# The first modulation's weights and the first norm's sums, in a hybrid diffusion trunk on Trainium2

## The chip, the cores and the metric

The program runs on one core of a Trainium2 chip. The metric is the device time of one execution in microseconds (us); lower is better. The engines are named as in the profile: PE (TensorE, matmuls), ACT (ScalarE), DVE (VectorE), POOL (GpSimd) and SP (SyncE, which issues loads).

## The reference

Two layers are computed for 128 context tokens and 512 latent tokens (640 together), with 1024 features, in float32. Only the beginning of the first layer is touched by the change:

```python
def modulation(cvec, w, b):
    m = jax.nn.silu(cvec) @ w + b
    return jnp.split(m[:, None, :], N_MOD, axis=-1)
...
sh1_p, sc1_p, g1_p, sh2_p, sc2_p, g2_p = modulation(c_ctx[None, :], mod_w, mod_b)
sh1_s, sc1_s, g1_s, sh2_s, sc2_s, g2_s = modulation(c, mod_w, mod_b)
hp = rms_norm(xp, norm1) * (1 + sc1_p) + sh1_p
hs = rms_norm(xs, norm1) * (1 + sc1_s) + sh1_s
```

`rms_norm` divides each token by the root of the mean of its squares over the 1024 features. The normed and modulated tokens go into one projection to queries, keys and values, then into attention, and so on through an MLP and a second layer.

## The kernel before

Tokens lie along the free axis and features along the 128 partitions: x is eight blocks (k = 0 to 7) of 128 x 640. A value that enters a large matmul is split into a rounded part, hi, and the rest, lo, so that each product is three matmuls (hi hi, hi lo, lo hi; lines 245 to 247 for the dense layers, 618 to 620 for `proj_step`).

The program has two phases. The first holds the attention layer; there a planner orders the instructions of each engine and of each queue by a timeline of its own, so that an instruction whose inputs and buffers are ready can be put ahead of one that was written earlier. The second phase (MLP, second layer) keeps the written order. The queues (SP's and ACT's loads among them) run in the order given to them. A load takes one of eight completion counters in turn and waits for the load that had that counter before.

`first_norm` (line 310) makes the eight blocks of hi and lo for the projection:

- It loads the eight x blocks on SP's queue (line 320), then the first 2048 columns of the modulation weights in four quarters w0 to w3 of 512 columns, 2 MB each (line 324), into three buffers, so that w3 waits for the buffer of w0. Behind w1 the call `use(None, None)` loads the first 256 projection columns, those of the keys and values (`proj_w`, line 608; line 611 is the load).
- `sumsq` (lines 295 to 299) squares each block on ACT and adds it into one tile `acc` on DVE. `rsqrt` (lines 306 to 308) multiplies `acc` by a matrix of ones, one matmul for each half of 320 tokens, which sums over the partitions and gives every partition the sum; Ln and Exp turn it into `rs`.
- For each quarter s, 32 small products (line 340, two records each) give the shifts and scales of blocks 2s and 2s + 1, a copy (343), a transpose (345) and a few tiny operations (348, 350) put them in place as the gain `g` and the shift.
- Then blocks 2s and 2s + 1 are scaled, shifted and split. Blocks 0 to 3 use one form: x times gain times `rs` on DVE (357), the rounded part with the shift added on ACT (358), the rest on DVE (359). Blocks 4 to 7 use another: x times `rs` on DVE (363), gain and shift on ACT for even blocks (369) and on DVE for odd ones (366), then a cast on ACT (235) and a subtract on DVE (236).
- `use(k, ...)` multiplies the block at once with the key/value columns, for five token blocks: 15 matmuls into three of the four `pj` banks of PSUM. The fourth, and the two `md` banks after the last modulation product, take the next 256 columns, which `proj` loads, splits and multiplies.

After it the kv banks are evacuated: `split_v` (605, 606), `qknorm` (681 to 686) and `rotated` (700 to 708), which needs tables built from `rope` (loaded on ACT's queue at line 662, used at 668 and 673). `cka` and `cv` (713, 715) are the context keys and values of the same stage, `vall` (711) holds the values. The pools `m0` (w) and `np` (acc, sq, rs) are closed when `first_norm` ends, and the memory behind the earlier tiles is then given to the pools `qkv`, `akq` and `qt` in this order; `rope` is the first tile of `qt`.

Of the kernel before, what the change touches and what calls it, by code (L numbers as in the profile page):

```python
# [18 lines left out]
P = 128  # L19
D = 1024  # L20
# [29 lines left out]
class Net:  # L50
# [259 lines left out]
    def first_norm(self, use):  # L310
# [3 lines left out]
        with ExitStack() as c:  # L314
# [3 lines left out]
            for k in range(NK):  # L318
                t = self.xp.tile([P, T], F32, tag="x", name="x")
                nc.sync.dma_start(out=t, in_=self.i["xT"][k * P:(k + 1) * P, :])  # L320
                xt.append(t)
            for s in range(4):
                wt = mp.tile([P, NK, 512], F32, tag="w", name="w")
                nc.sync.dma_start(out=wt, in_=w[:, s * 512:(s + 1) * 512].rearrange("(k p) c -> p k c", p=P))
                ws.append(wt)
                if s == 1:
                    use(None, None)
            for k in range(NK):
                self.sumsq(k, xt[k], 0, T)
            rs = self.np.tile([P, T], F32, tag="rs", name="rs", bufs=1)  # L330
            for hf in range(2):
                self.rsqrt(rs, hf, "kq")
            g = self.gain[0, 0]
            by_block = lambda z: z.rearrange("p (i k) -> p k i", i=2)
            for s in range(4):
# [11 lines left out]
                for v in range(2):  # L347
# [3 lines left out]
                                                   in1=self.vec("n1_0")[:, two], op0=ALU.add, op1=ALU.mult)  # L351
                for k in (2 * s, 2 * s + 1):
                    if k < 4:
                        x, (hi, lo) = xt[k], self.act[2 * k:2 * k + 2]
                        for v, o in ((0, slice(0, TS)), (1, slice(TS, T))):
                            sh = self.mod_vec(0, 0, k, v)
                            nc.vector.scalar_tensor_tensor(out=x[:, o], in0=x[:, o], scalar=g[:, k, v:v + 1], in1=rs[:, o], op0=ALU.mult, op1=ALU.mult)
                            nc.scalar.activation(hi[:, o], x[:, o], AF.Identity, bias=sh)
                            nc.vector.scalar_tensor_tensor(out=lo[:, o], in0=x[:, o], scalar=sh, in1=hi[:, o].bitcast(F32),
                                                           op0=ALU.add, op1=ALU.subtract)  # L360
                        use(k, (hi, lo))
                        continue
# [1382 lines left out]
```

## Time and profile before

| | us |
|---|---|
| three runs | 1806.48, 1808.74, 1809.97 |
| their median | 1808.74 |
| the profiled execution | 1806.72 |
| its span, from the first to the last instruction | 1805.0 |
| PE busy in it | 1726.7 |
| DVE, ACT busy in it | 1266.6, 921.0 |

The page of the profile gives the busy time of each engine over the whole span. The stretch that matters here is the first 60 us, so most of the reading is done with views that take a window: busy time by stretch, the timeline, the loads. Matmuls are pipelined, and their ends are modelled; a few per cent of the matmul records can be missing.

### The profile page before, as it was taken

The numbers are of one execution on the slowest core, as the hardware profiler recorded it, in microseconds if no ns is written. First come the engines' busy times: TensorE is split into PE (matmuls) and PEld (weight loads), VectorE is DVE, ScalarE is ACT, GpSimd is POOL, SyncE is SP. The second block draws the span as 40 slices with busy tenths as digits, with TensorE's granted clock in tenths as the row PEclk, the third lists the DMA queues.
The fourth block names the chain that finished last, engine by engine and source line by source line (L and its number), as shares of the span: only waits on it lengthen the run. The fifth ranks groups of instructions, "written<-read, shape, count | busy, mean of one in ns | idle before, by whom it ended". The sixth has DMA issues, their size and how long they took to land. (4 is left out here: it accounts for less than half of the span.)

```text
span 1805.0 us, 34898 instructions
## 1 busy us (share of the span) xinstructions
PE 1726.7 (96%) x14120; PEld 1621.2 (90%) x14120; DVE 1266.6 (70%) x2554; ACT 921.0 (51%) x2037; POOL 215.1 (12%) x218
## 2 busy tenths in 40 slices
PE   5999998899999999999989999999999999999999
PEld 4898886699999999999888878878999999999999
DVE  6766557469988678787697877776449957465562
ACT  4555565345345171554756656656636427164360
POOL 0233314100000000000232222222110000000000
PEclk9999998999999999999999999999999999999999
DMA  9101059314433435254122222232232423222231
GB/s 351 57 27 50 26 157 284 132 52 164 164 117 125 135 101 200 73 178 162 48 48 70 50 48 69 51 82 73 66 129 94 140 63 101 72 71 94 68 104 52
DMA packets 174994, 187.22 MB, mean 104 GB/s; under 512 B 48457, under 2 KB 152137, under 8 KB 174833
## 3 DMA queue, kind: packets, MB, share of 16 engines
q1 hardware_dynamic: 170272, 175.05, 30.9%
q0 software_dynamic: 1408, 5.41, 0.9%
q10 hardware_dynamic: 3152, 4.52, 0.8%
q8 instruction: 111, 1.82, 0.4%
q14 instruction: 51, 0.41, 0.1%
HBM read 170.97 MB, written 11.37 MB: 101 GB/s over the span
## 5 line engine op out<-in xcount | busy, mean ns | idle before, releaser
L228 ACT CAST t<-t 128x1024 fp32r<-128x1024 f32 x169 | 176.5, 1048 | 243.0 <-PE p L246 135.7
L229 DVE TENSOR_TENSOR t<-t 128x1024 fp32r<-128x1024 f32 x169 | 207.3, 1230 | 56.8 <-ACT t L228 55.9
L245 PE MATMUL dn<-t 128*128 128x320 f32 x648 | 207.7, 320 | 3.7 <-PEq L78 3.1
L246 PE MATMUL dn<-t 128*128 128x320 f32 x648 | 208.2, 321 | 0.0
L247 PE MATMUL dn<-t 128*128 128x320 f32 x648 | 207.4, 320 | 0.0
L246 PE MATMUL p<-hl,t 128*128 128x320 f32 x448 | 138.5, 309 | 0.0
L245 PEld LDWEIGHTS dn<-t 128*128 128x128 f32 x648 | 122.5, 189 | 7.9 <-issue 5.8
L246 PE MATMUL dn<-hl,t 128*128 128x320 f32 x416 | 129.0, 310 | 0.0
L192 DVE SCALAR_TENSOR_TENSOR ma<-t,ma 128x1024 f32<-128x1024 f32 x98 | 122.8, 1279 | 6.0 <-DMA t<-in_mod_w_dram 5.8
L246 PEld LDWEIGHTS dn<-t 128*128 128x128 f32 x648 | 122.6, 189 | 4.0 <-issue 2.5
L247 PEld LDWEIGHTS dn<-t 128*128 128x128 f32 x648 | 122.6, 189 | 3.4 <-issue 2.5
L413 DVE SCALAR_TENSOR_TENSOR x<-p,t,x 128x192 f32<-128x192 f32 (+2 forms) x154 | 53.1, 385 | 101.0 <-PE p L247 101.0
L245 PE MATMUL p<-hh,t 128*128 128x320 f32 x392 | 121.3, 310 | 0.0
L247 PE MATMUL p<-hh,t 128*128 128x320 f32 x392 | 121.2, 309 | 0.0
L245 PE MATMUL dn<-hh,t 128*128 128x320 f32 x376 | 116.8, 311 | 0.0
L247 PE MATMUL dn<-hh,t 128*128 128x320 f32 x376 | 116.2, 309 | 0.0
L228 ACT CAST wxh<-t 128x1024 fp32r<-128x1024 f32 x49 | 51.3, 1047 | 85.9 <-PE p L246 40.6
L413 DVE SCALAR_TENSOR_TENSOR x<-dn,t,x 128x320 f32<-128x320 f32 (+1 forms) x86 | 44.9, 525 | 62.4 <-PE dn L247 51.8
L246 PEld LDWEIGHTS p<-hl,t 128*128 128x128 f32 x448 | 84.1, 188 | 0.0
L246 PEld LDWEIGHTS dn<-hl,t 128*128 128x128 f32 x416 | 78.1, 188 | 1.0 <-issue 0.8
L783 POOL TENSOR_TENSOR p<-p,smx 128x640 f32<-128x640 f32 (+1 forms) x48 | 63.8, 1338 | 114.9 <-DVE smx L782 99.3
L245 PEld LDWEIGHTS p<-hh,t 128*128 128x128 f32 x392 | 73.6, 188 | 0.8 <-issue 0.4
(599 smaller groups left out, 5195.7 us busy)
## 6 DMA issues: line engine op xcount, KB each, us to landing
t<-in_mlp_w_dram SPq DMA_DIRECT2D x64, 1024.0 KB
t<-in_mod_w_dram SPq DMA_DIRECT2D x40, 1024.0 KB, 6.4
t<-in_w_qkv_dram SPq DMA_DIRECT2D x12, 1024.0 KB
t<-in_w_in_dram SPq DMA_DIRECT2D x9, 1024.0 KB, 5.4
w<-in_mod_w_dram SPq DMA_DIRECT2D x4, 2048.0 KB, 16.3
t<-in_w_out_dram SPq DMA_DIRECT2D x8, 1024.0 KB, 5.7
bias<-in_biasx_dram SPq DMA_DIRECT2D x8, 512.0 KB, 6.7
t<-in_w_z_dram SPq DMA_DIRECT2D x4, 1024.0 KB
```

Source lines behind the costliest of these rows:

```text
L192: nc.vector.scalar_tensor_tensor(out=acc[v], in0=wt[:, k], scalar=c, in1=acc[v], op0=ALU.mult, op1=ALU.add)
L228: nc.scalar.copy(hi, raw)
L229: nc.vector.tensor_tensor(out=lo, in0=raw, in1=hi.bitcast(F32), op=ALU.subtract)
L245: self.nc.tensor.matmul(ps, lhsT=hi[:, k, :], rhs=xh[:, ts_], start=(k == 0), stop=False)
L246: self.nc.tensor.matmul(ps, lhsT=hi[:, k, :], rhs=xl[:, ts_], start=False, stop=False)
L247: self.nc.tensor.matmul(ps, lhsT=lo[:, k, :], rhs=xh[:, ts_], start=False, stop=(k == NK - 1))
L413: nc.vector.scalar_tensor_tensor(out=xout[:, a:b], in0=ps[:, a - o:b - o], scalar=self.mod_vec(layer, idx, k, v), in1=xin[:, a:b], op0=ALU ...
L783: nc.gpsimd.tensor_tensor(out=pv, in0=pv, in1=sm.unsqueeze(2).broadcast_to([P, nb, w]), op=ALU.mult)
```

## The change

It touches `first_norm` and two loads in `attn_layer`. The first quarter of the modulation weights is loaded ahead of the x blocks, the projection columns come behind x, and the other three quarters behind them. The first modulation product is written ahead of the sums. The squares of blocks (0, 1), (2, 3) and (4, 5) are added in pairs on DVE, those of 6 and 7 are left single, and each of the five results is multiplied by the ones matrix into two PSUM banks that accumulate. `acc` is gone, `sq` has four buffers instead of two. All eight blocks use the form of blocks 0 to 3. The loads of `cka` and `cv` move from ACT's queue to SP's.

```diff
--- before.py
+++ after.py
@@ -315,24 +315,16 @@
             mp = c.enter_context(self.tc.tile_pool(name="m0", bufs=3))
             self.open_norm(c)
             xt, ws = [], []
-            for k in range(NK):
-                t = self.xp.tile([P, T], F32, tag="x", name="x")
-                nc.sync.dma_start(out=t, in_=self.i["xT"][k * P:(k + 1) * P, :])
-                xt.append(t)
-            for s in range(4):
+            g = self.gain[0, 0]
+            by_block = lambda z: z.rearrange("p (i k) -> p k i", i=2)
+
+            def load(s):
                 wt = mp.tile([P, NK, 512], F32, tag="w", name="w")
                 nc.sync.dma_start(out=wt, in_=w[:, s * 512:(s + 1) * 512].rearrange("(k p) c -> p k c", p=P))
                 ws.append(wt)
-                if s == 1:
-                    use(None, None)
-            for k in range(NK):
-                self.sumsq(k, xt[k], 0, T)
-            rs = self.np.tile([P, T], F32, tag="rs", name="rs", bufs=1)
-            for hf in range(2):
-                self.rsqrt(rs, hf, "kq")
-            g = self.gain[0, 0]
-            by_block = lambda z: z.rearrange("p (i k) -> p k i", i=2)
-            for s in range(4):
+
+            def modulation(s):
+
                 two = slice(2 * s, 2 * s + 2)
                 ps = self.bank("md")
                 for k in range(NK):
@@ -349,26 +341,44 @@
                                             in1=by_block(self.vec("modb0")[:, 0:16])[:, two], op=ALU.add)
                     nc.vector.scalar_tensor_tensor(out=g[:, two, v], in0=self.modT[0][:, 8 + 2 * s:10 + 2 * s, v], scalar=1.0,
                                                    in1=self.vec("n1_0")[:, two], op0=ALU.add, op1=ALU.mult)
+
+            load(0)
+            for k in range(NK):
+                t = self.xp.tile([P, T], F32, tag="x", name="x")
+                nc.sync.dma_start(out=t, in_=self.i["xT"][k * P:(k + 1) * P, :])
+                xt.append(t)
+            use(None, None)
+            for s in range(1, 4):
+                load(s)
+            modulation(0)
+
+            sums = [self.bank("kq")[:, 0:TH] for _ in range(2)]
+            for ks in ((0, 1), (2, 3), (4, 5), (6,), (7,)):
+                sq = []
+                for k in ks:
+                    sq.append(self.np.tile([P, T], F32, tag="sq", name="sq", bufs=4))
+                    nc.scalar.activation(sq[-1], xt[k], AF.Square)
+                if len(ks) == 2:
+                    nc.vector.tensor_tensor(out=sq[0], in0=sq[0], in1=sq[1], op=ALU.add)
+                for hf in range(2):
+                    nc.tensor.matmul(sums[hf], lhsT=self.ones, rhs=sq[0][:, hf * TH:(hf + 1) * TH], start=(ks[0] == 0), stop=(ks[0] == 7))
+            rs = self.np.tile([P, T], F32, tag="rs", name="rs", bufs=1)
+            for hf in range(2):
+                c = rs[:, hf * TH:(hf + 1) * TH]
+                nc.scalar.activation(c, sums[hf], AF.Ln, bias=self.eps, scale=1.0 / D)
+                nc.scalar.activation(c, c, AF.Exp, scale=-0.5)
+            for s in range(4):
+                if s:
+                    modulation(s)
                 for k in (2 * s, 2 * s + 1):
-                    if k < 4:
-                        x, (hi, lo) = xt[k], self.act[2 * k:2 * k + 2]
-                        for v, o in ((0, slice(0, TS)), (1, slice(TS, T))):
-                            sh = self.mod_vec(0, 0, k, v)
-                            nc.vector.scalar_tensor_tensor(out=x[:, o], in0=x[:, o], scalar=g[:, k, v:v + 1], in1=rs[:, o], op0=ALU.mult, op1=ALU.mult)
-                            nc.scalar.activation(hi[:, o], x[:, o], AF.Identity, bias=sh)
-                            nc.vector.scalar_tensor_tensor(out=lo[:, o], in0=x[:, o], scalar=sh, in1=hi[:, o].bitcast(F32),
-                                                           op0=ALU.add, op1=ALU.subtract)
-                        use(k, (hi, lo))
-                        continue
-                    nc.vector.tensor_tensor(out=xt[k], in0=xt[k], in1=rs, op=ALU.mult)
+                    x, (hi, lo) = xt[k], self.act[2 * k:2 * k + 2]
                     for v, o in ((0, slice(0, TS)), (1, slice(TS, T))):
-                        if k % 2:
-                            nc.vector.tensor_scalar(out=xt[k][:, o], in0=xt[k][:, o], scalar1=g[:, k, v:v + 1],
-                                                    scalar2=self.mod_vec(0, 0, k, v), op0=ALU.mult, op1=ALU.add)
-                        else:
-                            nc.scalar.activation(xt[k][:, o], xt[k][:, o], AF.Identity, scale=g[:, k, v:v + 1], bias=self.mod_vec(0, 0, k, v))
-                    use(k, self.split_act(k, xt[k]))
-            self.acc = None
+                        sh = self.mod_vec(0, 0, k, v)
+                        nc.vector.scalar_tensor_tensor(out=x[:, o], in0=x[:, o], scalar=g[:, k, v:v + 1], in1=rs[:, o], op0=ALU.mult, op1=ALU.mult)
+                        nc.scalar.activation(hi[:, o], x[:, o], AF.Identity, bias=sh)
+                        nc.vector.scalar_tensor_tensor(out=lo[:, o], in0=x[:, o], scalar=sh, in1=hi[:, o].bitcast(F32),
+                                                       op0=ALU.add, op1=ALU.subtract)
+                    use(k, (hi, lo))
         return [self.act[2 * k:2 * k + 2] for k in range(NK)]
 
     def norm_half(self, xt, layer, which, hf, tag="s1"):
@@ -710,9 +720,9 @@
 
             nc.scalar.dma_start(out=vall[:, 5, :], in_=I["ctxv"][:, 128:640])
             ck = tp.tile([P, KVA, 128], F32, name="cka", bufs=1)
-            nc.scalar.dma_start(out=ck, in_=I["ctxk"][:, 0:KVA])
+            nc.sync.dma_start(out=ck, in_=I["ctxk"][:, 0:KVA])
             cv = tp.tile([P, 128], F32, name="cv", bufs=1)
-            nc.scalar.dma_start(out=cv, in_=I["ctxv"][:, 0:128])
+            nc.sync.dma_start(out=cv, in_=I["ctxv"][:, 0:128])
             split_v(va[5], cv)
             kd = [tp.tile([P, KVA, 2, HD], F32, name=f"ka{blk}", bufs=1) for blk in range(NB)]
```

## Rows read from the trace of the kernel before

**Rows 1.** The page, part 1: TensorE's busy time, share of the span, instructions.
```profile
PE 1726.7 (96%) x14120; PEld 1621.2 (90%) x14120; DVE 1266.6 (70%) x2554; ACT 921.0 (51%) x2037; POOL 215.1 (12%) x218
```

**Rows 2.** Windows of the start: stretch, length, busy (instructions), granted clock, DMA share, GB/s.
```profile
4.50:6.00 1.50, 0.00 (x0) 0.00 (x0) 1.50 (x9) 0.00 (x0) 0.00 (x0) 1.00 0.96 267
17.80:41.40 23.60, 18.79 (x267) 16.59 (x267) 16.96 (x38) 9.67 (x17) 0.00 (x0) 0.93 1.06 373
24.00:27.00 3.00, 2.58 (x50) 2.13 (x40) 2.04 (x5) 1.76 (x4) 0.00 (x0) 0.50 1.07 371
44.00:58.00 14.00, 14.00 (x119) 13.97 (x117) 7.11 (x23) 5.64 (x15) 0.51 (x2) 1.00 0.15 47
58.00:75.00 17.00, 15.50 (x126) 14.92 (x125) 16.31 (x47) 9.94 (x38) 7.19 (x15) 1.00 0.24 70
```

**Rows 3.** Timeline, 14 to 42 us: start, length, engine, line, operation, count.
```profile
14.66 2.50 PE L306 MATMUL kq<-acc,t 128*128 128x320 f32 x4 [14.66 <-DVE acc L299]
...
16.13 0.53 ACT L307 ACTIVATE rs<-kq,t 128x320 f32<-128x320 f32 x1 [2.61 <-PE kq L306]
...
17.20 0.53 ACT L307 ACTIVATE rs<-kq,t 128x320 f32<-128x320 f32 x1
...
17.83 3.20 PE L340 MATMUL md<-w,t 128*32 128x128 f32 x64 [0.67 <-DMA w<-in_mod_w_dram]
...
22.25 1.94 DVE L357 SCALAR_TENSOR_TENSOR x<-x,t,rs 128x512 f32<-128x512 f32 x4
23.04 1.97 ACT L358 ACTIVATE t<-x,t 128x512 fp32r<-128x512 f32 x4 [1.66 <-DVE x L357]
...
23.36 3.22 PE L340 MATMUL md<-w,t 128*32 128x128 f32 x64 [1.54 <-DMA w<-in_mod_w_dram]
...
26.24 1.99 ACT L228 CAST t<-t 128x1024 fp32r<-128x1024 f32 x2 [1.24 <-DMA t<-in_w_in_dram]
...
27.34 0.62 PE L618 MATMUL pj<-t 128*128 128x256 f32 x3 [0.75 <-ACT t L228]
...
41.54 1.95 PE L340 MATMUL md<-w,t 128*32 128x128 f32 x64 [1.09 <-DMA w<-in_mod_w_dram]
```

**Rows 4.** Windows of the pj tiles alone, TensorE: busy time (matmuls) to 41.40.
```profile
0.00:41.40 41.40, 9.66 (x72) 0.96 1.00 353
```

**Rows 5.** DMA issues to 60 us: tile, queue, count, KB of each, median us to landing.
```profile
w<-in_mod_w_dram SPq DMA_DIRECT2D x4, 2048.0 KB, 16.3
t<-in_w_in_dram SPq DMA_DIRECT2D x4, 1024.0 KB, 14.7
x<-in_xT_dram SPq DMA_DIRECT2D x8, 320.0 KB, 6.1
rope<-in_rope_dram ACTq DMA_DIRECT2D x1, 256.0 KB, 2.8
...
cka<-in_ctxk_dram ACTq DMA_DIRECT2D x1, 128.0 KB, 3.3
cv<-in_ctxv_dram ACTq DMA_DIRECT2D x1, 64.0 KB, 5.0
```

**Rows 6.** Groups of ScalarE to 50 us, shapes apart: busy, mean ns, idle before.
```profile
L298 ACT ACTIVATE sq<-x 128x640 f32<-128x640 f32 x7 | 5.1, 736 | 1.5 <-DVE acc L299 0.8 <-DMA x<-in_xT_dram 0.8
...
L358 ACT ACTIVATE t<-x,t 128x512 fp32r<-128x512 f32 x4 | 2.8, 724 | 4.0 <-DVE x L357 4.0
```

**Rows 7.** Timeline of ScalarE and VectorE: rope's tables, a late load, the first kv evacuation.
```profile
4.43 0.42 DVE L668 TENSOR_TENSOR tbgqa_r<-rope,t 128x256 f32<-128x256 f32 x1 [0.40 <-DMA t<-in_vecs_dram]
...
5.65 0.62 DVE L673 TENSOR_TENSOR tbgkan_r<-rope,t 128x64 f32<-128x64 f32 x4
...
43.69 0.33 ACTq L711 DMA_DIRECT2D vall<-in_ctxv_dram  x1
...
53.66 0.27 ACT L605 CAST va<-pj 128x128 fp32r<-128x128 f32 x1 [5.81 <-PE pj L620]
...
57.44 0.29 DVE L700 TENSOR_TENSOR t<-kn,tbgkan_r 128x128 f32<-128x128 f32 x1
```

## The prediction

> **What bounds the kernel now.** I read the page first. TensorE (PE) is busy for 96% of the span [rows 1], so time is won only where PE idles, or where its work starts sooner. The windows show where it idles [rows 2]: 18.79 us busy of the 23.6 us from 17.80 to 41.40, and full, 14.00 of 14.00, from 44 to 58. In the first of these stretches the DMA engines' share is 1.06 at 373 GB/s: the start is bound by loading. The timeline shows in which order the loads let PE go [rows 3]. The sums of squares run at 14.66, each quarter w0 to w3 of the modulation product when its 2 MB land (17.83, 23.36, ..., 41.54), and the first key/value (kv) matmul at 27.34, as soon as the first 256 projection columns are cast (26.24; ACT had waited for that load). From 41.54 on PE has no gap; so the end of this stage is set by when w3 lands and by how many projection matmuls are left then. By 41.40, 72 of them were done [rows 4]; 119 matmuls in 14.00 us [rows 2] make 0.118 us for each one left.
>
> **The change, part by part.** *The order of loads.* Sizes are in [rows 5]: w 2.10 MB each, x 8 × 0.33, projection columns 1.05 each. The old queue had x, w0, w1, columns; the new one has w0, x, columns, w1, w2, w3. Ahead of the end of the first columns there are 2.10 MB (w1) and 0.45 MB (rope, cka, cv, if none of them stays in front) less: 2.55 MB at 373 GB/s are 6.8 us, so 26.2 becomes 19.4. Between 4.5 and 6.0 only 267 GB/s were moved [rows 2], while SP issued the eight small x loads; with 2 MB in front of them I expect the full rate, 0.16 MB or 0.4 us won: 19.0. By the same count w0 lands at 9.2 (6.2 MB less than the 8.3 that stand ahead of 26.2), the last x at 16.2 (3.6 MB less).
>
> w3 must wait for the buffer of w0 (three buffers). That is free once the first product is done, at about 13, so SP is not held there. But the planner, which puts each queue's instructions in the order in which they can run, had already put the second projection columns ahead of w3, and I expect it again; then the bytes ahead of w3 are the old ones less those of rope (0.26 MB, 0.7 us; see below). w3 lands 0.4 + 0.7 = 1.1 us sooner, at 40.4. Bounds: 0 (nothing won), and 3.9 (w3 ahead of those columns: another 1.05 MB, 2.8 us). I take 1.1, the order that the planner chose before.
>
> *The sums of squares.* Seven adds into acc on DVE become three; two ones-matmuls become ten. Two took 2.50 us, and their readers started 1.07 apart (16.13 and 17.20) [rows 3]; the first modulation product took 3.20 us against 1.95 for the fourth, so that pace is that of the lower level, 1.2 GHz. Ten cost 10.7 us at it, 5.4 at 2.4 GHz. They follow the first product (9.2 + 3.2 = 12.4), so they end between 18.7 (set by the last x at 16.2, its square of 0.74 [rows 6], a short queue and the last pair) and 23.1. I take 18.7, because PE then has work from 9.2 on with few gaps. After it come Ln and Exp (1.07 for each half by the two readers' distance, the first half partly under the last matmul, so some 1.6), the scale of block 0 (0.79, from 22.25 to 23.04) and its rounding (0.72 [rows 6]) with the handing over: the first kv matmul at 22.0 instead of 27.34. At worst it is 26.5.
>
> A rule of the Trainium skill speaks against this part: TensorE: Matmul & The Clock Gate, "Loop structure matters more than you think", calls a DMA wait between matmuls the bad loop, which leaves the array at the lower clock. By that rule the sums take the 10.7 us (cold sums, below). The trace agrees so far that the second product, after PE's wait for w1, took 3.22 us and the clock was granted at 0.50 from 24 to 27 [rows 2, 3].
>
> *What PE gets done before w3.* From 22.0 to 40.4 are 18.4 us. Off go the second and third product (1.95 each; w1 now lands at about 24.5) and one wait: from the end of a product to the first rounded block were 2.7 us (21.03 to 23.04 + 0.72 [rows 3, 6]), and blocks 0 and 1 are used up by then. An estimate of 0.5 for the two small transposes and their hand-overs goes off too. That leaves 11.3 us, or 95 matmuls, 23 more than the 72; at 0.118 that is 2.7 us. Bounds: with the sums at 1.2 GHz 13.9 us remain (26.5 to 40.4), less one product and 1.3 to 2.3 us of gaps, so 82 to 90: 1.2 to 2.1 us. At most 108 can be done (kv for six blocks, and the one block of the next columns that has a free bank): 4.2 us.
>
> *One form for all blocks.* Blocks 4 to 7 lose an early multiply by rs, a cast and a separate subtract, and take what blocks 0 to 3 had: 2.8 us for two blocks to be scaled and rounded (22.25 to 25.01 [rows 3]). The work on the last two blocks after w3 stays near its present length, and PE has the projections of the second columns (36 matmuls, 4.2 us, on the two md banks) to fill it: 0. If that filler had been used up, 2.8 us would show.
>
> *cka and cv* go from ACT's queue to SP's, 0.19 MB [rows 5], and wait behind w2 there, but in front of w3; nothing reads them before the last blocks are done: 0. At worst w3 is 0.5 us later than I count, were they moved from behind it.
>
> *Rope.* It is untouched, but its place is not. The tiles of this stage took 3 × 16 KB for w and 4 × 2.5 KB for acc, two sq and rs, 58 KB; the pools that come after (vall to kha) take 60, and rope begins behind them, so it was loaded at the start and its tables were built from 4.43 to 6.27 [rows 7]. Now there are four sq and rs: 60.5 KB. The last tile, rs, would reach into rope, and its load may only start when rs is read for the last time, at about 46 (40.4 + 1.95 + 2.7 for the first of the last two blocks, and the rest of them). For such an overlap the trace has an example: vall lies over w0's buffer, and its load was issued at 43.69, 0.2 us behind the end of the last product on it (41.54 + 1.95 [rows 3, 7]). Loads of this size landed 2.8 to 5.0 us after their issue [rows 5]. So rope lands at 49 to 51 and the tables (1.84 us of DVE) are ready near 52. The first rotation was at 57.44 [rows 7], and would now come near 53.6. It fits by a hair; I take 0, and the other end is the slower rival.
>
> **The sum.** 1.1 + 2.7 = 3.8 us less. The profiled execution took 1806.72 (span 1805.0), 2.0 below the median of 1808.74; from it comes 1802.9, and from the median **1804.9**. Its own range goes from 1.1 + 1.2 to 1.1 + 4.2: 1803.4 to 1806.4. Beyond 41 us PE was full until 58, so the lead is passed on, unless the planner shifts later work. About 0.2%, 3.6 us, is what can be told from no change, so this case lies on that line.
>
> **The rivals.** *A larger gain.* ACT waited 5.81 us, until 53.66, for the first finished kv bank [rows 7], while PE ran other projections. Then DVE was busy 16.31 of 17 us [rows 2]. If all six early blocks are in the banks before w3 lands, the evacuation starts up to 5.8 us sooner and DVE, the next limit there, with it: 1808.7 - 5.8 = 1802.9. For it: 22.0 is early. Against it: the planner interleaves.
>
> *Cold sums.* Each pair of ones-matmuls waits for its x blocks, PE's clock stays at 1.2 GHz as it did in the first product, and kv starts near 26.5: only 1.1 + 1.2 to 1.1 + 2.1 remain, about 1806.
>
> *Slower.* The rope load is issued by ACT, in order. If it stands behind the first copy out of a kv bank, which waited until 53.66, it lands near 58.5, the tables are ready at 60.4 instead of being there at 57.44, and their 1.84 us fall into the stretch where DVE has 0.7 us to spare: 3.0 + 1.84 = 4.8 us of loss, and PE's lead is then of no use: 1813.5. The point is whether the tables are ready when the first key is normed (57.44 now). Against it: the planner can put the issue before that copy.
>
> *It does not do what it says.* The planner leaves x ahead of w0, since all are ready at the start: 1808.7.
>
> **How the numbers follow.** Forecast 0.42, half of it beyond the line; larger gain 0.24; cold sums 0.12; slower 0.18; not done 0.04. Faster: 0.21 + 0.24 = 0.45; same: 0.21 + 0.12 + 0.04 = 0.37; slower 0.18. The range reaches from 1799, below the larger gain by the 3.9 us that w3 could come sooner, to 1813, nearly the whole of the slower case.
>
> **What would show it.** In the new timeline: the first product near 9.2, the last ones-matmul by 18.7, the first kv matmul near 22, the last product at 40.4, more than 90 matmuls into the pj banks before it, rope issued after the last scale and its tables done before the first rotation. I am wrong if the last product comes no sooner than 41, if PE idles after it, or if DVE stands at a rope table while a finished bank waits.

## The result and the profile after

The changed kernel took 1822.98 us in the median of four runs (1821.73 to 1825.38), the kernel before 1807.61 (1805.56 to 1809.97, four runs): a ratio of 1.0085, 95% interval 1.0066 to 1.0103. It is slower by 15 us where a gain was forecast, and lies above the predicted range (1799 to 1813). The profiled execution of the changed kernel took 1824.09 us with a span of 1822.4.

By the page's first part PE is busy for 13.5 us longer than in [rows 1] (1726.7), and idle for 3.9 us longer (82.2 of the span for 78.3). Of the longer busy time 4.4 us are the sums (3.47 and 3.40 us in the timeline below, for the 2.50 of before).

```profile
PE 1740.2 (95%) x14136; PEld 1629.8 (89%) x14136; DVE 1264.4 (69%) x2554; ACT 917.8 (50%) x2037; POOL 215.4 (12%) x218
```

The windows that answer to [rows 2] (stretch, length, busy time of PE, PEld, DVE, ACT and POOL with instructions, granted clock, DMA share, GB/s):

```profile
4.50:6.00 1.50, 0.00 (x0) 0.00 (x0) 0.00 (x0) 0.00 (x0) 0.00 (x0) 1.00 1.05 406
17.80:41.40 23.60, 18.27 (x208) 15.30 (x207) 13.91 (x32) 10.14 (x21) 0.00 (x0) 0.86 1.03 365
...
44.00:58.00 14.00, 14.00 (x140) 13.47 (x134) 7.27 (x29) 3.52 (x10) 0.00 (x0) 1.00 0.44 129
58.00:75.00 17.00, 12.63 (x92) 12.06 (x90) 15.40 (x46) 10.26 (x37) 5.84 (x14) 0.90 0.04 9
...
24.58:29.00 4.42, 4.42 (x38) 3.70 (x39) 2.23 (x6) 1.16 (x3) 0.00 (x0) 0.50 1.06 389
```

From 17.80 to 41.40 PE was busy for 0.5 us less than before and at a lower granted clock (0.86 for 0.93). From 44 to 58 it is full as before; behind that, from 58 to 75, it lacks 2.9 us of work.

The timeline of PE (start, length, line, operation, count; in brackets the idle time before and what ended it), which answers to [rows 3]:

```profile
9.90 3.64 PE L332 MATMUL md<-w,t 128*32 128x128 f32 x64 [9.90 <-DMA w<-in_mod_w_dram]
13.47 3.47 PE L364 MATMUL kq<-sq,t 128*128 128x320 f32 x8
...
16.89 3.40 PE L364 MATMUL kq<-sq,t 128*128 128x320 f32 x12
24.58 0.58 PE L628 MATMUL pj<-t 128*128 128x256 f32 x1 [4.30 <-ACT t L378]
...
26.15 1.92 PE L332 MATMUL md<-w,t 128*32 128x128 f32 x28
...
31.62 1.28 PE L332 MATMUL md<-w,t 128*32 128x128 f32 x36
...
33.53 1.95 PE L332 MATMUL md<-w,t 128*32 128x128 f32 x64
...
42.01 1.06 PE L332 MATMUL md<-w,t 128*32 128x128 f32 x26
...
43.67 0.64 PE L332 MATMUL md<-w,t 128*32 128x128 f32 x14
...
47.54 0.86 PE L332 MATMUL md<-w,t 128*32 128x128 f32 x24
...
49.15 0.27 PE L337 MATMUL md<-t,modm 128*128 128x128 f32 x1
...
62.73 0.33 PE L745 MATMUL kq<-t,ka 128*128 128x128 f32 x1 [3.24 <-DVE ka L718]
```

The loads did what was predicted: the first product at 9.90 instead of 17.83, the first kv matmul 2.8 us sooner than the 27.34 of before. But the second product, one piece at 23.36 before, begins at 26.15 and is cut in two by the kv matmuls of blocks 0 and 1; and the last, one piece at 41.54 before, is cut in three and ends at 48.40 instead of 43.49. PE has no gap there: it did kv matmuls in between. What the lead was meant to buy did not come either, as the window of the pj tiles shows (72 matmuls in [rows 4]):

```profile
0.00:41.40 41.40, 10.58 (x68) 0.92 0.98 346
```

The other engines pass the delay on. ACT and VectorE, answering to [rows 3, 7]:

```profile
19.43 1.99 ACT L228 CAST t<-t 128x1024 fp32r<-128x1024 f32 x2 [1.63 <-DMA t<-in_w_in_dram]
...
51.84 0.36 ACTq L672 DMA_DIRECT2D rope<-in_rope_dram  x1
...
55.10 0.50 ACT L609 CAST kha<-cka 128x128 fp32r<-128x128 f32 x2 [2.48 <-DMA cka<-in_ctxk_dram]
...
57.01 0.27 ACT L615 CAST va<-pj 128x128 fp32r<-128x128 f32 x1 [1.17 <-PE pj L630]
```

```profile
34.04 1.94 DVE L377 SCALAR_TENSOR_TENSOR x<-x,t,rs 128x512 f32<-128x512 f32 x4
...
49.86 1.94 DVE L377 SCALAR_TENSOR_TENSOR x<-x,t,rs 128x512 f32<-128x512 f32 x4
...
57.47 0.62 DVE L683 TENSOR_TENSOR tbgkan_r<-rope,t 128x64 f32<-128x64 f32 x4
...
61.40 0.29 DVE L710 TENSOR_TENSOR t<-kn,tbgkan_r 128x128 f32<-128x128 f32 x1
```

The rows of before that these are compared with, for blocks 2 and 3, the last transpose and the first key:

```profile
29.98 1.94 DVE L357 SCALAR_TENSOR_TENSOR x<-x,t,rs 128x512 f32<-128x512 f32 x4
...
44.48 0.27 PE L345 MATMUL md<-t,modm 128*128 128x128 f32 x1
...
58.78 0.33 PE L735 MATMUL kq<-t,ka 128*128 128x128 f32 x1 [0.60 <-DVE ka L708]
```

Blocks 2 and 3 are scaled at 34.04 (29.98 before), blocks 6 and 7 at 49.86 (45.41), the first kv bank is evacuated at 57.01 (53.66), the first key rotated at 61.40 (57.44). PE has done its spare projections by 59.5 and waits 3.24 us for that key, at a time when it had waited 0.60 before (until 58.78).

From there the delay grows. SP's loads mark how far the kernel has come: the first of the last four pieces of projection columns (line 255), and the first weights of the MLP, where the written order begins. Before, then after:

```profile
83.18 78.36 SPq L255 DMA_DIRECT2D t<-in_w_in_dram  x4
...
366.42 10.67 SPq L255 DMA_DIRECT2D t<-in_mlp_w_dram  x2
```

```profile
90.83 79.49 SPq L255 DMA_DIRECT2D t<-in_w_in_dram  x4
...
381.44 10.29 SPq L255 DMA_DIRECT2D t<-in_mlp_w_dram  x2
```

That is 3.4 us late at the first evacuation, 7.7 at 90.83 and 15.0 at the MLP, of 17.4 between the two spans. So most of the loss arises in the first phase; 2.4 us lie behind it, in code that the change does not touch.

### The profile page after: what moved, and what is told of

Its sections match the earlier page's. It is cut to its first block, busy times and chain, and to the rows that moved or that the text cites. A ratio compares the mean times of both kernels' runs of the same rounds, so it can differ in the third digit from the quotient of the medians.

```text
span 1822.4 us, 34919 instructions
## 1 busy us (share of the span) xinstructions
PE 1740.2 (95%) x14136; PEld 1629.8 (89%) x14136; DVE 1264.4 (69%) x2554; ACT 917.8 (50%) x2037; POOL 215.4 (12%) x218
## 4 chain that ended last, share of the span: by engine, by line
PE 59%; DVE 12%; ACT 4%; DMA 3%; issue 2%; POOL 0%; DVEq 0%; ACTq 0%; POOLq 0%; SPq 0%
PE dn L245 7%; PE dn L246 7%; PE dn L247 7%; PE dn L484 6%; PE p L247 5%; PE p L245 5%; PE p L246 5%; PE s L484 4%; PE p L484 4%; DVE ma L192 3%; DMA t<-in_mlp_w_dram 1%; DMA t<-in_mod_w_dram 1%; DVE t L229 1%; PE p L1450 1%; PE p L1459 1%
## 5 line engine op out<-in xcount | busy, mean ns | idle before, releaser
L229 DVE TENSOR_TENSOR t<-t 128x1024 fp32r<-128x1024 f32 x169 | 207.6, 1232 | 56.9 <-ACT t L228 55.8
```

What stands on the lines that cost most here:

```text
L229: nc.vector.tensor_tensor(out=lo, in0=raw, in1=hi.bitcast(F32), op=ALU.subtract)
```

## The experiments

The theories, as the expectations name them. **P** (place): `rs`, the tile of the root, reaches into the memory of rope's pool, so that rope, cka and cv are loaded late. **Q**: the last product in pieces. **K**: the new load order; with the columns ahead of w1 there is kv work early, the planner puts it ahead of and between the products, and w1 and w2 come later. K1 puts this down to the order on PE, K2 to the loads. **W**: w0 ahead of x makes x late. **S**: the matmuls with ones. **O**: one form for all blocks. **N**: any new order of the plan costs something by itself. Each kernel ran beside the kernel before on the same chip (medians there 1808.9 to 1810.5 us). The columns of the table: ratio of the times with its interval, first kv evacuation and first MLP load in the profiled execution.

| kernel | ratio | kv evacuation | MLP load |
|---|---|---|---|
| before | 1 | 53.66 | 366.42 |
| changed | 1.0085 [1.0066, 1.0103] | 57.01 | 381.44 |
| a_sq3 | 1.0100 [1.0073, 1.0127] | 61.66 | 385.30 |
| b_sq3 | 1.0033 [1.0019, 1.0046] | 56.08 | 371.85 |
| a_hoist | 1.0063 [1.0042, 1.0084] | 54.74 | 375.31 |
| a_sq3_hoist | 1.0058 [1.0036, 1.0081] | 56.12 | 375.88 |
| a_w1 | 1.0049 [1.0027, 1.0072] | 52.80 | 368.82 |
| b_w0 | 1.0109 [1.0079, 1.0140] | 59.66 | 379.80 |
| b_kv | 1.0044 [1.0028, 1.0060] | 57.58 | 371.39 |
| a_ahead | 1.0047 [1.0029, 1.0065] | 53.60 | 372.16 |
| b_kv_ahead | 1.0041 [1.0026, 1.0057] | 57.95 | 374.51 |
| b_w0_w1_ahead | 1.0053 [1.0036, 1.0071] | 55.73 | 372.36 |
| b_psum | 1.0012 [1.0000, 1.0025] | 54.42 | 366.66 |
| b_one | 1.0038 [1.0021, 1.0055] | 53.86 | 367.73 |
| a_sq3_w1_act | 1.0028 [1.0017, 1.0039] | 53.43 | 365.47 |
| a_sq3_w1_act_ahead | 1.0012 [1.0001, 1.0024] | 54.63 | 366.50 |
| b_ahead | 1.0028 [1.0016, 1.0040] | 53.42 | 372.77 |

**The place of the root.** a_sq3 is the changed kernel with three square buffers, which keeps the root out of rope's pool; b_sq3 is the kernel before with a third buffer, which puts it in.

```diff
-                    sq.append(self.np.tile([P, T], F32, tag="sq", name="sq", bufs=4))
+                    sq.append(self.np.tile([P, T], F32, tag="sq", name="sq", bufs=3))
```

> The changed kernel with three buffers for the squares instead of four, so that rs ends where it ended before and the pool of rope, cka and cv is free from the start. Theory P (place: 480 bytes of rs in that pool make rope, cka and cv wait for the last scale, and that is the main loss): most of the 15 us come back, 1807 to 1811. Theory Q (the order: the last modulation product now stands in three pieces between kv matmuls, ends near 48 instead of 43.5, and the kv banks are finished later while PE has used up its other work): the loads are early again, but the product is still in pieces, so only the 2 us of table work and the wait for cka come back: 1817 to 1821.

Measured 1827.45 us (1823.17 to 1830.06). That is above the range of either theory. Rope was loaded at 0.83 and its tables built at 4.22, yet the kernel is no faster than the changed one: P is not the main cause. The order got worse besides, with the first product at 12.25 instead of 9.90 and the last in five pieces from 45.80 to 53.04.

```diff
-        sq = self.np.tile([P, T], F32, tag="sq", name="sq", bufs=2)
+        sq = self.np.tile([P, T], F32, tag="sq", name="sq", bufs=3 if self.first else 2)
```

> The kernel before with a third buffer for the squares and nothing else: rs lies 2.5 KB further, 480 bytes of it in the pool of rope, cka and cv. Theory P alone: the loads come after the last scale and the time is 8 to 15 us longer, 1816 to 1823. Theory Q: the last product stays in one piece, so the time is within 4 us of before, 1807 to 1812.

Measured 1815.01 us (1809.93 to 1819.56), between the range of Q (to 1812) and that of P (from 1816). Rope was issued at 31.68 and its tables were built from 44.69 on; the evacuation came at 56.08. The overlap, or the new order that it brings, costs a third of a per cent, in a kernel whose last product is still one piece at 41.81.

**The last product in one piece.** a_hoist writes the last product right behind the third one; a_sq3_hoist has the three buffers besides.

```diff
-                if s:
-                    modulation(s)
+                if s == 1:
+                    modulation(1)
+                if s == 2:
+                    modulation(2)
+                    modulation(3)
```

> The changed kernel with the last modulation product written ahead of blocks 4 and 5, so that PE does it in one piece; the places in memory are as in the changed kernel. Theory Q: the last product ends by 43 to 44, the first kv bank is evacuated 3 to 4 us sooner, 1809 to 1814. Theory P: the pool still waits for the last scale, which itself comes 4 us sooner, so at most that is won: 1817 to 1822.

Measured 1819.92 us (1817.49 to 1822.97). The last product is whole, 64 records at 42.00, and its transpose comes at 46.63 instead of 49.15, the evacuation at 54.74. That is 2.3 us sooner, where Q had 3 to 4, and the time lies in the range of P and not in Q's: a miss for Q. About a quarter of the loss goes (0.0085 to 0.0063, with intervals that overlap).

```diff
-                    sq.append(self.np.tile([P, T], F32, tag="sq", name="sq", bufs=4))
+                    sq.append(self.np.tile([P, T], F32, tag="sq", name="sq", bufs=3))
...
+                if s == 2:
+                    modulation(2)
+                    modulation(3)
```

> Both edits together: three buffers for the squares, and the last product in one piece. If P and Q are the two causes and nothing else is, this has the gain that was forecast: 1803 to 1807. If the cause lies in the sums or in the one form for all blocks, it stays above 1811.

Measured 1818.56 us (1815.61 to 1826.54), a miss: both repairs together do not bring the time back. The second product was still in two pieces (26 and 38 records, at 27.61 and 33.43). So something ahead of the last product had to be looked for.

**The columns behind w1 again.** a_w1 undoes one line of the change.

```diff
-            use(None, None)
             for s in range(1, 4):
                 load(s)
+                if s == 1:
+                    use(None, None)
```

> The changed kernel with the first projection columns loaded behind w1 again, as before the change; all else as changed. Theory K (the columns ahead of w1 give PE filler, kv matmuls, before the second product is there; the planner then puts the products in pieces between and behind the filler, and the last blocks come late): the second and the last product run in one piece, the second ends by 27, the last by 44; 1809 to 1815, with the 4 us of the third-buffer run still in it. Theory O (the one form for blocks 4 to 7, longer on DVE, is the cause): stays at 1818 to 1823.

Measured 1817.57 us (1815.38 to 1822.46), between the ranges of K (to 1815) and O (from 1818). In its PE timeline the second and the last product are whole again and begin when their weights land:

```profile
22.01 2.50 PE L332 MATMUL md<-w,t 128*32 128x128 f32 x64 [2.02 <-DMA w<-in_mod_w_dram]
...
40.31 1.95 PE L332 MATMUL md<-w,t 128*32 128x128 f32 x64 [0.53 <-DMA w<-in_mod_w_dram]
```

The evacuation comes at 52.80, 0.9 us sooner than in the kernel before, and yet the time is half a per cent above it.

**The load order alone.** b_w0 is the kernel before with the new order of loads (w0, x, columns, w1, w2, w3) and the first product written ahead of the sums; sums, forms and the other queues are as before.

```diff
+            load(0)
             for k in range(NK):
...
+            use(None, None)
+            for s in range(1, 4):
+                load(s)
+            modulation(0)
```

> The kernel before with the new order of loads and the first product written ahead of the sums (w0, x, columns, w1, w2, w3), and nothing else: sums on DVE, two forms, old queues. Theory K: this alone brings most of the loss, 1816 to 1823, with the second product after 30. Theory O: 1805 to 1811.

Measured 1829.11 us (1822.41 to 1832.93), the slowest of all by its median. Its products are cut as in the changed kernel (62 and 2 records; 10, 36, 16 and 2), and the evacuation comes at 59.66. So the load order by itself brings the whole loss, and more than K had given it (to 1823); that the other parts of the change give some of it back is not shown, since the intervals of 1.0109 and 1.0085 overlap.

**The columns alone.** b_kv is the kernel before with the first columns ahead of w1 and nothing else.

```diff
-                if s == 1:
+                if s == 0:
                     use(None, None)
```

> The kernel before with one edit: the first step's columns are loaded ahead of w1 instead of behind it. x still comes ahead of w0, sums and forms are as before. Theory K1: with the columns there early the planner has kv matmuls to put ahead of the products, and in the order of the program the second product stands in two pieces (28 and 36 records) with the kv matmuls of two blocks between, the last one also in two; first kv evacuation at 55 to 58 us, ratio 1.003 to 1.009, time 1812 to 1825. Rival W (what costs is that w0 goes ahead of x and so x lands later): this kernel is within 0.2 per cent of before, 1806 to 1811, with the evacuation at 53 to 54.5 us.

Measured 1817.67 us (1814.40 to 1820.33), as K has it. The pj tiles' window to 41.40, PE's timeline, and VectorE's row for blocks 2 and 3:

```profile
0.00:41.40 41.40, 9.17 (x59) 1.00 1.00 353
```

```profile
26.34 0.58 PE L618 MATMUL pj<-t 128*128 128x256 f32 x1 [2.56 <-ACT t L358]
...
27.50 1.92 PE L340 MATMUL md<-w,t 128*32 128x128 f32 x28
...
33.11 1.28 PE L340 MATMUL md<-w,t 128*32 128x128 f32 x36
...
43.09 1.52 PE L340 MATMUL md<-w,t 128*32 128x128 f32 x48
...
45.44 0.64 PE L340 MATMUL md<-w,t 128*32 128x128 f32 x16
```

```profile
35.58 1.94 DVE L357 SCALAR_TENSOR_TENSOR x<-x,t,rs 128x512 f32<-128x512 f32 x4
```

The kv matmuls start 1.0 us sooner than before (27.34), and by 41.40 there are 59 of them instead of 72. The second product ends at 34.39 instead of 26.58, so blocks 2 and 3 are scaled at 35.58 instead of 29.98, and their work comes after the third product, where it stands ahead of the last. Columns ahead of w1 buy 1.0 us at the head and cost 5.6 us in the middle.

**Products written one step ahead.** a_ahead is the changed kernel with all its loads, sums and its form, but with product s + 1 written ahead of the blocks of step s.

```diff
-                if s:
-                    modulation(s)
+                if s < 3:
+                    modulation(s + 1)
```

> The changed kernel with all of its loads, sums and its one form, but each modulation product is written one step ahead: product s+1 stands before the blocks of step s, so that the planner has it to place first. In the order of the program the third product's 64 records and the fourth's then stand in one piece each, with fewer kv matmuls ahead of them. Theory K1 (the loss comes from the order that the planner gives PE, products behind and between kv matmuls, not from when the weights land): the last product ends by 44 us instead of 49, the first kv evacuation comes at 53.5 to 55.5 us (57.0 after the change, 53.7 before), and the time is 1811 to 1818. Theory K2 (the loss comes from the loads themselves: columns ahead of w1 make w1 to w3 land later whatever the order): second product not before 26 us, the evacuation stays at 56 to 58 us, time 1820 to 1825. Theory P (tables that wait for the place of the root): the tables still start at 51.8 us, the first rotation stays past 60 us, time 1820 to 1825.

Measured 1818.16 us (1813.80 to 1823.85). No load is touched, and every product is whole:

```profile
26.31 3.64 PE L332 MATMUL md<-w,t 128*32 128x128 f32 x64
...
33.10 1.96 PE L332 MATMUL md<-w,t 128*32 128x128 f32 x64
...
40.75 1.95 PE L332 MATMUL md<-w,t 128*32 128x128 f32 x64
```

The evacuation comes at 53.60, the MLP load at 372.16. Nearly half of the loss (0.85% to 0.47%) was the order that the written place of the products gives. The rope tables still came as late as 52.59, which speaks against P once more. K1 had also 1811 to 1818 for the time; the median lies 0.2 us above that.

b_kv_ahead asks the same of the kernel before: columns ahead of w1, products one step ahead.

```diff
+            load(0)
+            use(None, None)
...
+                if s < 3:
+                    modulation(s + 1)
```

> The kernel before with the first columns ahead of w1 (as in the run before with that alone) and each product written one step ahead of its blocks. Theory K1 (columns ahead of w1 cost through the order of the products): second product whole at 27 to 28 us, last product begun by 43 us, first kv evacuation at 53.5 to 55.5 us instead of 57.9, ratio 1.000 to 1.003. Theory K2 (they cost because w1 and w2 land later): the evacuation stays at 56.5 to 58 us and the ratio at 1.004 to 1.006.

Measured 1818.01 us (1814.16 to 1821.29): the figures are those of K2. The second product is whole at 27.31 and ends near 30.5, but the blocks that wait for it are not scaled any sooner. Its VectorE timeline:

```profile
33.29 0.23 DVE L340 TENSOR_TENSOR t<-md,t 128x4 f32<-128x4 f32 x2 [4.90 <-PE md L337]
36.33 1.23 DVE L229 TENSOR_TENSOR t<-t 128x1024 fp32r<-128x1024 f32 x1 [2.81 <-ACT t L228]
37.47 0.22 DVE L342 SCALAR_TENSOR_TENSOR t<-t 128x2 f32<-128x2 f32 x2
37.66 1.94 DVE L368 SCALAR_TENSOR_TENSOR x<-x,t,rs 128x512 f32<-128x512 f32 x4
```

Between the shift (L340) and the gain (L342) of blocks 2 and 3 stands the split of the second columns (L229), whose load landed only at 35.25 (the cast on ACT had waited 4.30 us for it); VectorE stands 2.81 us at it. By this trace the loss with early columns comes from the order on all engines, not on PE alone: a whole product is not enough when the transpose behind it (32.98) or VectorE's next step waits for something else. No run moved that split, so this reading is argued. That w1 itself lands too late is not shown: nothing on PE waited for it.

**w0 ahead of x.** b_w0_w1_ahead takes the kernel before, puts w0 ahead of x and the first product ahead of the sums, leaves the columns behind w1, and writes the products one step ahead.

```diff
+            load(0)
             for k in range(NK):
...
+                if s < 3:
+                    modulation(s + 1)
```

> The version that the earlier runs point to: the kernel before with w0 loaded ahead of x and the first product written ahead of the sums, the columns behind w1 as before, and each product written one step ahead of its blocks; sums by VectorE and two forms as before, tables on ScalarE's queue as before. Theory K1: products 2 and 3 are whole and nothing of kv stands in front of them that is not needed; last product by 41 us (44.5 before), first kv evacuation at 51.5 to 53.5 us, time 1801 to 1808. Rival W (x lands some 4 us later when w0 goes ahead, and all that waits for the root goes with it): evacuation at 54 to 57 us, time 1812 to 1820.

Measured 1819.25 us (1816.45 to 1820.66): W is right, K1's forecast for it was not. The two matmuls with ones start 5.5 us later than at 14.66, about what the 2.10 MB of w0 take (5.4 us at the 389 GB/s of the window above); PE, then VectorE:

```profile
20.14 2.50 PE L306 MATMUL kq<-acc,t 128*128 128x320 f32 x4 [3.33 <-DVE acc L299]
```

```profile
23.75 1.94 DVE L369 SCALAR_TENSOR_TENSOR x<-x,t,rs 128x512 f32<-128x512 f32 x4 [3.66 <-ACT rs L308]
```

Blocks 0 and 1 are scaled at 23.75 instead of 22.25, blocks 2 and 3 at 33.05 instead of 29.98. With the sums on VectorE, w0 ahead of x only moves the wait from w0 to x. Part of the 0.53% is the order of the products: b_ahead below differs from this kernel in the place of w0 alone and has 0.28% and 53.42, so w0 ahead of x costs some 0.25%, with intervals that overlap, and 2.3 us at the evacuation.

**The sums in PSUM alone**, in the kernel before, with three buffers for the squares.

```diff
-            for k in range(NK):
-                self.sumsq(k, xt[k], 0, T)
+            sums = [self.bank("kq")[:, 0:TH] for _ in range(2)]
+            for ks in ((0, 1), (2, 3), (4, 5), (6,), (7,)):
...
```

> The kernel before with the sums of squares taken in PSUM as the blocks come (three buffers for the squares, two banks), and nothing else: loads, queues and both forms as before, products in the order of before in the plan. Theory K1 says that this part is harmless by itself: the root comes some 1 to 2 us sooner, PE's first products hold it back where they share PE, the evacuation stays at 53 to 55 us, and the time is 1804 to 1811. Rival S (the ten matmuls with the 128x128 of ones in fp32, cold, delay the products and so the rest): 1812 to 1818, with the last product ending later than 44.5 us.

Measured 1811.70 us (1809.97 to 1816.56): 0.1%, which cannot be told from no change. The 20 records of the sums take 7.54 us in it, from 8.45 on, most of it in time in which PE had nothing to do before (its first matmul came at 14.66). The median lies between the ranges of K1 (to 1811) and S (from 1812), but the last product ends at 43.13, not later than 44.5 as S had it: S falls.

**One form alone**, in the kernel before: blocks 4 to 7 take the form of blocks 0 to 3.

```diff
-                    if k < 4:
...
-                    nc.vector.tensor_tensor(out=xt[k], in0=xt[k], in1=rs, op=ALU.mult)
...
-                    use(k, self.split_act(k, xt[k]))
+                    use(k, (hi, lo))
```

> The kernel before with one form for all blocks and nothing else. Theory K: within 4 us of before, 1807 to 1813. Theory O: 1815 to 1822, with the evacuation of the kv banks later than 56.

Measured 1815.19 us (1807.34 to 1820.96): the time is in the range of O, the evacuation (53.86) is not late as O had it. The profiled execution was the shortest of its ten runs (span 1805.6), so its views do not show where the 0.4% lies. At the evacuation 0.2 us are lost.

**The repaired change.** a_sq3_w1_act is the changed kernel with a_sq3, a_w1 and the two caches on ACT's queue as before; a_sq3_w1_act_ahead also has the products one step ahead. Both keep w0 ahead of x, the sums in PSUM and the one form.

```diff
-            nc.sync.dma_start(out=ck, in_=I["ctxk"][:, 0:KVA])
+            nc.scalar.dma_start(out=ck, in_=I["ctxk"][:, 0:KVA])
...
-            nc.sync.dma_start(out=cv, in_=I["ctxv"][:, 0:128])
+            nc.scalar.dma_start(out=cv, in_=I["ctxv"][:, 0:128])
```

> The changed kernel with three square buffers, the columns behind w1 and cka, cv on ACT's queue: what is left of the change is w0 ahead of x, the sums in PSUM and the one form. Theory K: no loss is left, 1803 to 1810. Theory O: 1814 to 1820. If the sums in PSUM cost, the second product is later than 26 and the time lies between.

Measured 1814.52 us (1811.46 to 1815.22): a miss for K, which had at most 1810, and in the range of O. The form for all blocks, with its 0.38% in b_one, is not cleared.

> The changed kernel with w0 ahead of x, sums in PSUM and one form kept, and with the columns behind w1 again, three buffers for the squares, the key and value caches on ScalarE's queue as before, and products written one step ahead. Theory K1: what is left of the change is w0 ahead of x, paid back in part by the earlier sums; first kv evacuation at 52.5 to 54.5 us, ratio 0.999 to 1.003. Rival W (x that lands later costs in full, as without the PSUM sums, where the ratio was 1.0053): evacuation at 55.5 to 57 us, ratio 1.004 to 1.007.

Measured 1812.48 us (1809.00 to 1815.53); the evacuation at 54.63 lies 0.1 us above K1's range, the ratio within it. Of the changed kernel's 0.85%, 0.73 go with the columns' place, the buffers, the queues and the written order of the products. What stays is w0 ahead of x, the sums in PSUM and the one form, and together they gain nothing; no run takes these three apart in this kernel. None of the kernels tried is faster than the kernel before.

**A new order alone.** b_ahead is the kernel before with all loads as they were and the products one step ahead.

```diff
+            load(0)
+            for s in range(1, 4):
+                load(s)
+                if s == 1:
+                    use(None, None)
+            modulation(0)
...
+                if s < 3:
+                    modulation(s + 1)
```

> The kernel before with all loads as they were; only the modulation products are written one step ahead of their blocks, so that the planner places each of them whole. Theory N (any new order of the plan costs some tenths of a per cent through the rest of the first phase, loads untouched): ratio 1.002 to 1.005, though the last product still ends at 43 to 44 us and the first kv evacuation comes at 53 to 54.5 us as before. Theory K1 (the order of the products is what counts, and the loads set the rest): the last product cannot come before its weights land at 41 us, so nothing is gained or lost: within 0.2 per cent of before, 1806 to 1813.

Measured 1814.77 us (1811.36 to 1821.39): the figures are those of N. The evacuation at 53.42 is no later than before, and the columns of line 255 are loaded at 83.82 (83.18); the first load of the output weights, at 318.68 instead of 312.41, is 6.3 us late. The windows of before, then of b_ahead:

```profile
210.00:260.00 50.00, 47.15 (x298) 42.23 (x297) 23.82 (x33) 30.33 (x60) 9.35 (x11) 0.97 0.40 117
260.00:310.00 50.00, 42.73 (x357) 30.71 (x356) 39.03 (x74) 32.05 (x90) 18.92 (x19) 0.90 0.88 267
```

```profile
210.00:260.00 50.00, 47.15 (x299) 43.02 (x298) 25.39 (x35) 32.54 (x62) 10.11 (x11) 1.00 0.35 97
260.00:310.00 50.00, 39.59 (x319) 28.02 (x322) 33.56 (x62) 27.04 (x78) 15.46 (x17) 0.83 0.89 251
```

From 260 to 310 PE is busy for 3.1 us less in this execution, at a granted clock of 0.83 instead of 0.90, and the MLP load comes 6.4 us late. Such a price of some tenths of a per cent stands in most of the other ratios too: a_w1 and b_one lose 0.4 to 0.5% although their first evacuation comes 0.9 us sooner and 0.2 later than before. A rule for any new order it is not: the 0.12% of b_psum cannot be told from nothing.

## Why the prediction was wrong

*The order of loads* held: the first product was forecast for 9.2 and came at 9.90, the cast of the columns at 19.0 and came at 19.43. w3 was forecast for 40.4; in the changed kernel nothing waited for it, in a_w1, with the same bytes ahead of it but for the columns' place, it landed at 40.31.

*The sums of squares* were sized too low: they ended at 20.29 instead of 18.7. The product ahead of them took 3.64 us, the pace of the lower level (b_psum's second product, at 23.07, took 3.64 at a granted clock of 0.50), although the granted clock from 9.90 to 13.54 reads 1.00. Of the 20 records of the sums the first eight took 3.47 us; the last twelve, still to be done at 16.89, took 3.40, near the pace of the upper level. The 6.87 together lie between the 5.4 and 10.7 of the two levels. Ln and Exp of both halves stood behind the cast of the columns on ACT and ended at 22.98, and the first kv matmul came at 24.58 instead of 22.0, inside the bounds (26.5 at worst). Then PE, after 4.30 us without work, ran the kv matmuls 0.21 us apart at a granted clock of 0.50 until 29.00. The Trainium skill's rule from "TensorE: Matmul & The Clock Gate", "Loop structure matters more than you think", that a long wait between matmuls leaves the array cold, agrees with that row, though the wait here was for ACT; the 10.7 us that the sums would have taken by it were too long.

*What PE gets done before w3* is the step that failed. It counted 95 matmuls by filling the time from the first kv matmul to w3 and took off the products, one wait and some transposes. It let each product run when its weights land, and looked at what w1's later landing costs PE, not at who waits for it: blocks 2 and 3 need the second product, and so do all kv matmuls after the first 30. With early columns the second product was put into and behind the kv matmuls of blocks 0 and 1 (26.15 and 31.62), blocks 2 and 3 were ready 4.1 us later than before, and 68 matmuls were done instead of 72. The sentence "so the lead is passed on, unless the planner shifts later work" and the "Against it: the planner interleaves" name the risk without a price or a rival. What it came to: the planner put kv matmuls whose inputs were ready ahead of the last product, on which the last two blocks, and with them the end of the stage, depend, and the last transpose came 4.7 us later (49.15 for 44.48). b_kv shows the first in a kernel that is otherwise the one before, a_ahead the second with all loads unchanged. The prediction's own signs of being wrong came with it: the last product began at 42.01, no sooner than 41, PE idled behind it (3.24 us), and VectorE was at rope's tables until 58.09 while the first kv bank had been finished at 57.01.

*One form at 0* was right for this stage (b_one's evacuation is at 53.86), and wrong by some 7 us for the whole (0.38%); no view shows where these lie.

*Rope, cka and cv* went much as the slower rival had it (tables at 60.4, 1813.5 us): the loads at 51.84 and later, ACT 2.48 us at the cache, the tables done at 58.09. The 0 for cka and cv failed with it: they did not load ahead of w3 but with rope, behind the last scale (51.87 and 52.26). But the rotation would have been late without this: a_sq3, with the tables at 4.22, is no faster, and the same overlap alone costs 0.33% in b_sq3. The rival had the right sign, and a cause that accounts for less than half of the loss.

*Beyond 60 us* the prediction passed a lead or a loss on one for one. A 3.4 us loss at the evacuation became 15.0 at the MLP load, and b_ahead, with none, lost 6.4. Nor does all of the loss lie ahead of that load. The windows from the first MLP load to the end, of before, a_w1 and a_sq3_w1_act, hold the same written instructions:

```profile
366.42:1805.00 1438.58, 1407.45 (x11648) 1343.86 (x11646) 1039.92 (x2104) 718.99 (x1569) 118.85 (x112) 1.00 0.31 96
368.82:1813.60 1444.78, 1410.93 (x11642) 1345.41 (x11640) 1037.96 (x2104) 718.54 (x1569) 118.12 (x112) 1.00 0.31 96
365.47:1810.00 1444.53, 1410.84 (x11643) 1345.99 (x11642) 1039.10 (x2104) 718.95 (x1569) 118.47 (x112) 1.00 0.31 96
```

Of the 8.6 us by which the span of a_w1 is longer, 6.2 lie in this stretch; a_sq3_w1_act is 0.9 us ahead of the kernel before at the MLP load and 5.0 behind it at the end. Over the 17 profiled executions the stretch took 1437.9 to 1448.9 us. What costs this, in the later part of the first phase and in the second, is not settled. The late blocks are not the whole loss either: a_ahead and a_w1, whose evacuation is no later than before, still lose 0.47 and 0.49%, so little more than two fifths of the 0.85% came back with it.

## What to carry to other kernels

Where a planner or a scheduler fills an engine with whatever is ready, an earlier load is no gain by itself: ask which work it makes ready, and whether that work stands in front of the one step on which the last blocks wait. Follow a load that is moved back to all who wait for its result, not only to the engine that reads it. Before a gain of 0.2% is claimed for a stage, measure what an edit without any such effect costs: here a new order alone cost 0.28%.

## What the runs showed of the hardware

Runs of one program differ together with their mean granted clock. Over the 75 runs of the kernel before that stood beside the experiments, the six with a mean of 0.994 had a median of 1805.9 us, the ten with 0.989 one of 1811.9; a straight line through all gives 1.3 us for each 0.001. The four runs of the changed kernel had 0.987 to 0.989, where the 75 had 0.991 in the mean; by that line some 4 of the 15 us go with the clock. Which of the two is the cause, a clock that falls because PE idles more or a PE that is later because the clock falls, was not tried.
